# Mixing layers of a hybrid stack: four split weight pieces begun a layer ahead instead of two, and two high parts kept in the tiles of the attention's turned weights

## The chip, the cores and the metric

One core of a Trainium2 chip runs one program. The metric is the time of the device in microseconds (us); of several executions the median is given. PE is TensorE, DVE VectorE, ACT ScalarE, POOL GpSimd, SP SyncE.

## The reference, cut to what matters

The reference is a stack of four token mixers (attention, mLSTM, HGRN2, attention) on 272 tokens, and then two blocks on 256 tokens, each of which mixes tokens and then applies a feed-forward part. The change lies at the entry of the two mixing parts:

```python
for l in range(DEPTH_2):                     # 2
    h = rmsnorm_2(x, g_pre_mix[l])
    z = jnp.einsum('bsd,de->bse', h, w_in[l])
    ...                                      # z is split; MoBA, FoX, MLA and dilated attention
    y = jnp.einsum('bse,ed->bsd', mix, w_out[l])
    x = x + rmsnorm_2(y, g_post_mix[l])
    h = rmsnorm_2(x, g_pre_ffn[l])
    f = jax.nn.silu(h @ w_gate[l]) * (h @ w_up[l])
    x = x + rmsnorm_2(f @ w_down[l], g_post_ffn[l])
```

All is float32. `D_MODEL` is 1024.

## The kernel before, in words

**Layers.** The program runs the layers a0, b, c, a3 and then M0, F0, M1, F1: a mixing layer M and a feed-forward layer F for each of the two blocks (`layer_mix` builds M). Activations lie with features on partitions: `HT` holds the residual stream as eight tiles of 128 features by tokens, k = 0 to 7.

**Precision.** Each float32 operand is split into a high part, rounded to float32r, and a low part, the rest. A product takes three matmuls: high weights by high activations (L402), high by low (L403), low by high (L404). The activations' parts are `XH` (an ACT instruction, L545) and `XL` (DVE, L533), one pair for each k.

**The stream of weights.** All weights are one stream of chunks, cut into pieces of 128 x 1024 (512 KB), numbered p; p0 below is the first piece of a mixing layer. A piece is split in one of two ways.

- From a raw copy: SP loads it to `wraw` (L258, 3 buffers), ACT casts it to the high part `whi` (L389), DVE subtracts to get the low part `wlo` (L395).
- "Parted": `begin_part` has POOL load the float32r copy `whi` (L329); `finish_part` has ACT write its negative to `wlo` (L336) and POOL add the piece from memory to it in the transfer (L337).

There are 7 buffers of `whi` (`WH`) and 5 of `wlo` (`WB`). The function `ahead` decides, at each piece, which parted pieces are begun and finished: `far, few, fewer = FAR` lets pieces up to 9 ahead be begun while at most 2 are begun or made, and one be finished early.

**A mixing layer.** Its first chunks, p0 and p1, and p2 and p3, go the way from a raw copy; chunk 3 does as well, but into tiles called `MH` and `ML`; from p6 on the pieces are parted. The generator `together` runs the first four products as one: for each k, the high parts of p0 to p3 by XH (4 matmuls), by XL (4), then the low parts by XH (4); 96 matmuls in all (L1576). All pieces of chunks 1 and 2 are in use until its last k. After it come the products of chunk 3 (`MH`, `ML`), then those of p6, p7 and so on.

**The norm at the entry.** M0 follows the last attention layer, whose last out-projection tiles are added to `HT` (DVE, L966). M1 follows F0: DVE computes the reciprocal root `RP`, PE spreads it, DVE scales `Y` (L1526), the sum goes into `HT` (L1527, k = 0 on DVE, the others on POOL), ACT makes XH, DVE makes XL. In both, ACT squares `HT` to `nsq` (L480), POOL adds these up (M0: L491 into `nsa`; M1: L485), and a few matmuls sum over features (M0: L495 and L496; M1: L456). In M0 their result scales the products; the products do not wait for it.

**Order.** The order on an engine is that in which the program issues the instructions, by a list of due times; each waits by semaphores for its operands and buffers. POOL issues its transfers in the same order as its additions.

**The attention's turned weights.** Later in a mixing layer `attend` keeps the transposed attention weights in two tiles, `pT0` and `pT1`, of 3 KB a partition together, two buffers each.

Of the kernel before, what the change touches and what calls it, by code (L numbers as in the profile page):

```python
# [9 lines left out]
F32 = mybir.dt.float32  # L10
F32R = mybir.dt.float32r
# [7 lines left out]
P = 128  # L19
# [40 lines left out]
WR, WH = 3, 7  # L60
HI_AHEAD, LO_AHEAD, FAR = 5, 3, (9, 2, 1)
PB = {"mm": 3, "s": 2, "t": 1, "g": 1, "a": 1}
# [161 lines left out]
def kernel(ctx: ExitStack, tc: tile.TileContext, xt: bass.AP, pos: bass.AP, small: bass.AP,  # L224
# [86 lines left out]

    parted, n_, off_, p_ = [], 0, 0, 0
    for i_, (t_, kt_, nt_) in enumerate(seq):
        first_ = i_ == 0 or t_ in ("bg", "c", "a3", "i0", "f0", "i1", "f1") and t_ != seq[i_ - 1][0] and seq[i_ - 1][0][:2] != "up"
        n_ = 1 if first_ else n_ + 1
        w_ = _cols(kt_, nt_)
        for x_, c0_ in enumerate(range(0, w_, SUB * P)):
            if POOL(t_, n_, x_) and not (n_ in MORE and t_[0] in MT):
                parted.append((p_, off_, w_, c0_, min(w_, c0_ + SUB * P)))
            p_ += 1  # L320
        off_ += P * w_
# [18 lines left out]
    def ahead(p, hold):  # L340


        far, few, fewer = FAR
        while parted and parted[0][0] <= p:
            begin_part()
        while begun and (begun[0][0] <= (p if hold else p + LO_AHEAD) or begun[0][0] <= p + far and not hold and len(made_lo) < fewer):
            finish_part()
        while parted and not hold and (parted[0][0] <= p + HI_AHEAD or parted[0][0] <= p + far and len(begun) + len(made_lo) < few):
            begin_part()
# [12 lines left out]
    def chunk(tag, into=None, more_due=False):  # L362
# [6 lines left out]
        for c0 in range(0, n, SUB * P):  # L369
# [11 lines left out]
            elif more:  # L381
                hi, lo = (t[:, c0:c0 + SUB * P] for t in acc["more"])
            else:
                hi = wp.tile([P, SUB * P], F32R, name="whi", bufs=WH)
                lo = wp.tile([P, SUB * P], F32R, name="wlo", bufs=WB)
# [1145 lines left out]
    def layer_mix(l, upd):  # L1531
# [3 lines left out]
        with tc.tile_pool(name=f"M{l}", bufs=2, reuse_waits="tile") as wk:  # L1535
            acc["more"] = [t.rearrange("p a b -> p (a b)") for t in mview(wk, 8, S)]
            Rf, _ = norm_in(wk, "gpm", 8 * l, NM, upd, CUT_S if upd else None)
            R = Rf[:, NM:]
# [160 lines left out]
            def attend(kind, mt, p, qf, vt):  # L1699
                pts = [wk.tile([P, 2, S], F32, name="pT0"), wk.tile([P, 2, P], F32, name="pT1")]  # L1700

# [436 lines left out]
```

## Time and profile before

| | |
|---|---|
| Median of 3 runs | 1419.31 us (1416.23 to 1421.89) |
| The profiled execution | 1422.77 us |
| Its span, first to last instruction | 1421.0 us |
| Mean granted TensorE clock | 0.993 |
| Busy: PE, DVE, ACT, POOL | 95%, 70%, 57%, 31% |

Times in the rows below are counted from the start of the span of that one execution. The time outside the span is 1.8 us. M0's `together` runs from 752.96 to 766.73, M1's from 1086.74 to 1098.67.

### The profile page before, as it was taken

To read this page: it belongs to the slowest core of one execution; us is meant where nothing else is said; L and a number is where in the kernel's file an instruction comes from. 1 tells how busy PE (TensorE), PEld (TensorE's weight loads), DVE (VectorE), ACT (ScalarE), POOL (GpSimd) and SP (SyncE) were. 2 spreads that over 40 slices of the span, in tenths; PEclk is the share of its full clock that TensorE was granted. 3 is DMA by queue.
4 is the path that set the end of the run, shared out by engine and by line. 5 is a ranking of instruction groups with operands and counts; after the bars stand their busy time and mean duration, and the time that the engine had idled before them with its cause. 6 is when DMAs were issued, how large, how long until landed. Compare 5 with 4: busy or idle time off the path is not lost.

```text
span 1421.0 us, 27398 instructions
## 1 busy us (share of the span) xinstructions
PE 1356.4 (95%) x10347; PEld 1261.1 (89%) x10347; DVE 992.2 (70%) x2424; ACT 804.6 (57%) x1700; POOL 446.6 (31%) x611
## 2 busy tenths in 40 slices
PE   6999999999899999998999999999999899999997
PEld 5878989999899888898778888999999789899986
DVE  5865569999776767687656676787645576687744
ACT  6875655556644454448675586454444667455532
POOL 3322468778703434123224511300014340400000
PEclk9999999999999999999999999999999999999999
DMA  9989999999568988559889973456564994466662
GB/s 275 283 186 209 230 242 247 231 238 242 135 185 234 253 180 196 134 179 247 191 171 237 259 193 104 144 189 195 180 198 151 265 239 125 119 193 194 186 184 89
DMA packets 79349, 281.88 MB, mean 198 GB/s; under 512 B 9024, under 2 KB 10184, under 8 KB 79216
## 3 DMA queue, kind: packets, MB, share of 16 engines
q0 software_dynamic: 44512, 160.74, 49.0%
q1 hardware_dynamic: 34272, 118.60, 26.0%
q8 instruction: 81, 1.33, 0.4%
q10 hardware_dynamic: 432, 0.79, 0.1%
q14 instruction: 52, 0.43, 0.1%
HBM read 279.01 MB, written 1.07 MB: 197 GB/s over the span
## 4 chain that ended last, share of the span: by engine, by line
PE 72%; DVE 10%; DMA 6%; ACT 5%; issue 4%; POOL 2%; SPq 0%; DVEq 0%; POOLq 0%; ACTq 0%
PE pmm L402 14%; PE pmm L403 14%; PE pmm L404 14%; DMA wraw<-in_wts_dram 2%; PE ps L404 2%; PE ps L403 2%; PE ps L402 2%; DVE wlo L395 2%; DMA wlo<-in_wts_dram 2%; PE ps L838 1%; DMA whi<-in_wts_dram 1%; PE pa L878 1%; PE ps L1270 1%; PE pt L863 1%; PE pmm L1893 1%
## 5 line engine op out<-in xcount | busy, mean ns | idle before, releaser
L402 PE MATMUL pmm<-XH,whi 128*128 128x272 f32 (+1 forms) x1544 | 458.1, 298 | 17.5 <-ACT whi L389 10.8
L404 PE MATMUL pmm<-XH,wlo 128*128 128x272 f32 (+1 forms) x1544 | 444.8, 289 | 8.5 <-DMA wlo<-in_wts_dram 7.9
L403 PE MATMUL pmm<-XL,whi 128*128 128x272 f32 (+1 forms) x1544 | 445.4, 289 | 2.6 <-DVE XL L533 2.6
L389 ACT CAST whi<-wraw 128x1024 fp32r<-128x1024 f32 (+1 forms) x211 | 217.8, 1033 | 242.5 <-DMA wraw<-in_wts_dram 180.4
L395 DVE TENSOR_TENSOR wlo<-wraw,whi 128x1024 fp32r<-128x1024 f32 (+1 forms) x211 | 256.5, 1217 | 96.5 <-PE pmm L404 43.3
L402 PEld LDWEIGHTS pmm<-XH,whi 128*128 128x128 f32 x1544 | 294.4, 191 | 31.7 <-ACT whi L389 10.8
L404 PEld LDWEIGHTS pmm<-XH,wlo 128*128 128x128 f32 x1544 | 294.9, 191 | 10.0 <-DMA wlo<-in_wts_dram 8.5
L403 PEld LDWEIGHTS pmm<-XL,whi 128*128 128x128 f32 x1544 | 295.0, 191 | 4.4 <-DVE XL L533 3.7
L336 ACT ACTIVATE wlo<-whi 128x1024 fp32r<-128x1024 f32 (+1 forms) x150 | 157.9, 1054 | 86.4 <-PE pmm L404 39.8
L337 POOL DMA_DIRECT2D wlo<-in_wts_dram x150 | 130.5, 873 | 212.3 <-ACT wlo L336 101.1
L402 PE MATMUL pmm<-MH,whi 128*128 128x256 f32 (+1 forms) x624 | 182.3, 292 | 0.6 <-DVE HT L966 0.6
L329 POOL DMA_DIRECT2D whi<-in_wts_dram x150 | 89.5, 598 | 296.7 <-PE pmm L404 235.9
L403 PE MATMUL pmm<-ML,whi 128*128 128x256 f32 (+1 forms) x624 | 177.9, 285 | 1.5 <-DVE ML L586 0.8
L404 PE MATMUL pmm<-MH,wlo 128*128 128x256 f32 (+1 forms) x624 | 177.3, 284 | 0.0
L402 PEld LDWEIGHTS pmm<-MH,whi 128*128 128x128 f32 x624 | 117.7, 189 | 7.8 <-issue 6.2
L403 PEld LDWEIGHTS pmm<-ML,whi 128*128 128x128 f32 x624 | 117.9, 189 | 2.2 <-DVE ML L586 1.1
L404 PEld LDWEIGHTS pmm<-MH,wlo 128*128 128x128 f32 x624 | 118.1, 189 | 0.0
L404 PE MATMUL ps<-XH,wlo 128*128 128x256 f32 (+1 forms) x256 | 72.5, 284 | 1.4 <-DVE wlo L395 1.4
L403 PE MATMUL ps<-XL,whi 128*128 128x256 f32 (+1 forms) x256 | 72.9, 285 | 0.0
L402 PE MATMUL ps<-XH,whi 128*128 128x256 f32 (+1 forms) x256 | 72.0, 283 | 0.0
L404 PEld LDWEIGHTS ps<-XH,wlo 128*128 128x128 f32 x256 | 48.7, 190 | 1.6 <-DVE wlo L395 1.6
L403 PEld LDWEIGHTS ps<-XL,whi 128*128 128x128 f32 x256 | 48.4, 189 | 0.0
(933 smaller groups left out, 2870.2 us busy)
## 6 DMA issues: line engine op xcount, KB each, us to landing
wraw<-in_wts_dram SPq DMA_DIRECT2D x209, 512.0 KB, 4.4
whi<-in_wts_dram POOLq DMA_DIRECT2D x148, 512.0 KB, 6.4
wlo<-in_wts_dram POOLq DMA_DIRECT2D x148, 512.0 KB, 7.8
wraw<-in_wts_dram SPq DMA_DIRECT2D x16, 384.0 KB, 3.5
nb<-drb POOLq DMA_DIRECT2D x8, 272.0 KB, 6.4
HT<-in_xt_dram SPq DMA_DIRECT2D x4, 272.0 KB, 9.7
nb<-drf POOLq DMA_DIRECT2D x8, 128.0 KB, 4.9
whi<-in_wts_dram POOLq DMA_DIRECT2D x2, 384.0 KB, 6.9
```

Of the source, the lines that this page charges most:

```text
L329: nc.gpsimd.dma_start(hi[:, :c1 - c0], src)
L336: act(lo[:, :w], hi[:, :w].bitcast(F32), AF.Copy, scale=-1.0)
L337: nc.gpsimd.dma_start(lo[:, :w], src, accum_op=ALU.add)
L389: nc.scalar.copy(hi[:, :c1 - c0], raw[:, :c1 - c0])
L395: V.tensor_tensor(lo[:, :c1 - c0], raw[:, :c1 - c0], hi[:, :c1 - c0].bitcast(F32), op=ALU.subtract)
L402: PE.matmul(ps, c.hi(b), xh, start=first, stop=False)
L403: PE.matmul(ps, c.hi(b), xl, start=False, stop=False)
L404: PE.matmul(ps, c.lo(b), xh, start=False, stop=last)
L838: PE.matmul(sv, qp[:, n, qs], kp[:, :, k0:k1], start=True, stop=False)
L863: PE.transpose(pt[:c1 - c0, (2 * y + x) * P:(2 * y + x + 1) * P], p_[:, x, c0:c1], K["ident"])
L878: PE.matmul(po[64 * x:64 * x + 64, :], vt[:kk, bq - 1 + y, 64 * x:64 * x + 64], pT[:kk, y, x].rearrange("p n t -> p (n t)"), start=y == 0, ...
L1270: PE.matmul(sl[:, 0:P], s["kw"], halves_of(kq, CB_[0], T + CA[0], b), start=True, stop=True)
```

## The change

The rule `FAR` becomes a pair: where the next piece to be begun belongs to a mixing layer (its tags begin with "i" or "u"), four pieces instead of two may be begun or made. Those begun take `whi` buffers while the layer ahead still runs. The high parts of chunk 2 (p2 and p3) no longer take `whi` buffers: they go into two tiles of the mixing layer's own pool, named `pT`, 4 KB a partition each. `attend` takes its two tiles of turned weights as views of one such tile.

```diff
--- before.py
+++ after.py
@@ -58,7 +58,7 @@
 WB = 5
 DV, UPP = (), True
 WR, WH = 3, 7
-HI_AHEAD, LO_AHEAD, FAR = 5, 3, (9, 2, 1)
+HI_AHEAD, LO_AHEAD, FAR = 5, 3, {False: (9, 2, 1), True: (9, 4, 1)}
 PB = {"mm": 3, "s": 2, "t": 1, "g": 1, "a": 1}
 BLOCKS = ((0, 16), (16, 144), (144, 272))
 CMASK = 7 * P + 64
@@ -309,7 +309,7 @@
                 tag[:2] == "up" and UPP or tag == "b" and (n, x) in B_PL or tag == "c" and n >= 3 and n % C_PN in C_PM or tag[0] == "f" and (n, x) in PF)
 
 
-    parted, n_, off_, p_ = [], 0, 0, 0
+    parted, mixing, n_, off_, p_ = [], set(), 0, 0, 0
     for i_, (t_, kt_, nt_) in enumerate(seq):
         first_ = i_ == 0 or t_ in ("bg", "c", "a3", "i0", "f0", "i1", "f1") and t_ != seq[i_ - 1][0] and seq[i_ - 1][0][:2] != "up"
         n_ = 1 if first_ else n_ + 1
@@ -317,6 +317,8 @@
         for x_, c0_ in enumerate(range(0, w_, SUB * P)):
             if POOL(t_, n_, x_) and not (n_ in MORE and t_[0] in MT):
                 parted.append((p_, off_, w_, c0_, min(w_, c0_ + SUB * P)))
+                if t_[0] in "iu":
+                    mixing.add(p_)
             p_ += 1
         off_ += P * w_
     begun, made_lo = [], {}
@@ -340,9 +342,9 @@
     def ahead(p, hold):
 
 
-        far, few, fewer = FAR
         while parted and parted[0][0] <= p:
             begin_part()
+        far, few, fewer = FAR[bool(parted) and parted[0][0] in mixing]
         while begun and (begun[0][0] <= (p if hold else p + LO_AHEAD) or begun[0][0] <= p + far and not hold and len(made_lo) < fewer):
             finish_part()
         while parted and not hold and (parted[0][0] <= p + HI_AHEAD or parted[0][0] <= p + far and len(begun) + len(made_lo) < few):
@@ -381,7 +383,10 @@
             elif more:
                 hi, lo = (t[:, c0:c0 + SUB * P] for t in acc["more"])
             else:
-                hi = wp.tile([P, SUB * P], F32R, name="whi", bufs=WH)
+                if tag[0] == "i" and state["n"] == 2:
+                    hi = acc["big"]()
+                else:
+                    hi = wp.tile([P, SUB * P], F32R, name="whi", bufs=WH)
                 lo = wp.tile([P, SUB * P], F32R, name="wlo", bufs=WB)
             with ExitStack() as es:
                 if (tag, state["n"], c0 // (SUB * P)) in HELD and "last" in acc:
@@ -1534,6 +1539,8 @@
         X = (XH, XL)
         with tc.tile_pool(name=f"M{l}", bufs=2, reuse_waits="tile") as wk:
             acc["more"] = [t.rearrange("p a b -> p (a b)") for t in mview(wk, 8, S)]
+
+            acc["big"] = lambda: wk.tile([P, SUB * P], F32R, name="pT", bufs=2)
             Rf, _ = norm_in(wk, "gpm", 8 * l, NM, upd, CUT_S if upd else None)
             R = Rf[:, NM:]
             mixed = []
@@ -1697,7 +1704,9 @@
                 fl.later(D_VT, turn)
 
             def attend(kind, mt, p, qf, vt):
-                pts = [wk.tile([P, 2, S], F32, name="pT0"), wk.tile([P, 2, P], F32, name="pT1")]
+                big = acc["big"]().bitcast(F32)
+                pts = [big[:, :2 * S].rearrange("p (x t) -> p x t", x=2),
+                       big[:, 2 * S:2 * S + 2 * P].rearrange("p (x t) -> p x t", x=2)]
 
                 def scores(b):
                     nk = P * (b + 1)
```

The count of instructions is the same on every engine. What moves lies at the entries of M0 and M1. The L-numbers of the changed kernel are higher by two to seven there (L331 is L329, L339 is L337, L338 is L336, L394 is L389, L400 is L395, L550 is L545, L538 is L533, L1583 is L1576, L1531 and L1532 are L1526 and L1527).

**First place: the entry of M0.** POOL there, before: two high parts begun in the layer a3, a third and fourth only when two are used, the low part of p6 after two additions, then four high parts ahead of the low parts of p7 and of those behind it.

```order
L329 DMA whi<-in_wts_dram 128x1024
L337 DMA wlo<-in_wts_dram 128x1024 x2
L329 DMA whi<-in_wts_dram 128x1024 x2
L491 TENSOR_TENSOR nsa<-nsq 128x256
L491 TENSOR_TENSOR nsa<-nsq,nsa 128x256
L337 DMA wlo<-in_wts_dram 128x1024
L491 TENSOR_TENSOR nsa<-nsq,nsa 128x256 x4
L329 DMA whi<-in_wts_dram 128x1024 x4
L337 DMA wlo<-in_wts_dram 128x1024 x4
L329 DMA whi<-in_wts_dram 128x1024
```

And in the changed kernel:

```order
L331 DMA whi<-in_wts_dram 128x1024
L339 DMA wlo<-in_wts_dram 128x1024
L331 DMA whi<-in_wts_dram 128x1024 x3
L496 TENSOR_TENSOR nsa<-nsq 128x256
L496 TENSOR_TENSOR nsa<-nsq,nsa 128x256 x3
L339 DMA wlo<-in_wts_dram 128x1024
L496 TENSOR_TENSOR nsa<-nsq,nsa 128x256 x2
L331 DMA whi<-in_wts_dram 128x1024 x2
L339 DMA wlo<-in_wts_dram 128x1024 x4
L331 DMA whi<-in_wts_dram 128x1024
```

Two of the high parts moved from behind the additions to ahead of them; two, not four, now stand ahead of the low part of p7. The low part of p6 moved behind two more additions.

ACT at the same place, before: the casts of p1, p2, p3 stand among the XH of the entry, the three squares behind them.

```order
L389 CAST whi<-wraw 128x1024
L545 ACTIVATE XH<-HT,sm 128x256 x2
L389 CAST whi<-wraw 128x1024
L545 ACTIVATE XH<-HT,sm 128x256 x3
L480 ACTIVATE nsq<-HT 128x256 x3
L545 ACTIVATE XH<-HT,sm 128x256
L336 ACTIVATE wlo<-whi 128x1024
L389 CAST MH<-wraw 128x1024 x2
L545 ACTIVATE XH<-HT,sm 128x256
L480 ACTIVATE nsq<-HT 128x256 x5
```

And in the changed kernel:

```order
L394 CAST whi<-wraw 128x1024
L550 ACTIVATE XH<-HT,sm 128x256
L394 CAST whi<-wraw 128x1024
L550 ACTIVATE XH<-HT,sm 128x256 x5
L485 ACTIVATE nsq<-HT 128x256 x3
L394 CAST pT<-wraw 128x1024 x2
L394 CAST MH<-wraw 128x1024
L550 ACTIVATE XH<-HT,sm 128x256
L485 ACTIVATE nsq<-HT 128x256 x3
L338 ACTIVATE wlo<-whi 128x1024
L485 ACTIVATE nsq<-HT 128x256
L394 CAST MH<-wraw 128x1024
```

The casts of p2 and p3, now into `pT`, moved behind the three squares, the second cast into `MH` behind the low part of p6 and a square.

**Second place: the entry of M1.** DVE there, before: nothing but the norm, since the low parts of p2 and p3 are made ahead of it.

```order
L449 SCALAR_TENSOR_TENSOR RP<-RP 128x2
L1526 SCALAR_TENSOR_TENSOR Y<-Y,sm,pg 128x256
L1527 TENSOR_TENSOR HT<-HT,Y 128x256
L1526 SCALAR_TENSOR_TENSOR Y<-Y,sm,pg 128x256 x2
L533 SCALAR_TENSOR_TENSOR XL<-HT,sm,XH 128x256
L1526 SCALAR_TENSOR_TENSOR Y<-Y,sm,pg 128x256
```

And in the changed kernel:

```order
L454 SCALAR_TENSOR_TENSOR RP<-RP 128x2
L1531 SCALAR_TENSOR_TENSOR Y<-Y,sm,pg 128x256
L400 TENSOR_TENSOR wlo<-wraw,pT 128x1024
L1532 TENSOR_TENSOR HT<-HT,Y 128x256
L1531 SCALAR_TENSOR_TENSOR Y<-Y,sm,pg 128x256 x2
L400 TENSOR_TENSOR wlo<-wraw,pT 128x1024
L538 SCALAR_TENSOR_TENSOR XL<-HT,sm,XH 128x256
L1531 SCALAR_TENSOR_TENSOR Y<-Y,sm,pg 128x256
```

The two subtractions moved into the chain from Y to HT and to XL.

PE towards the end of `together` in M1, before: the matmuls that sum the squares (L456) stand behind the first product with `MH`.

```order
L1576 MATMUL pmm<-XL,whi 128x256 x3
L1576 MATMUL ps<-XL,whi 128x256
L1576 MATMUL pmm<-XH,wlo 128x256 x3
L1576 MATMUL ps<-XH,wlo 128x256
L402 MATMUL ps<-XH,MH 128x256
L403 MATMUL ps<-XL,MH 128x256
L404 MATMUL ps<-XH,ML 128x256
L456 MATMUL pa<-ones,nsq 128x1 x4
L402 MATMUL ps<-XH,MH 128x256
L403 MATMUL ps<-XL,MH 128x256
```

And in the changed kernel, where L461 is L456 and L1583 is L1576:

```order
L1583 MATMUL ps<-XH,wlo 128x256
L1583 MATMUL pmm<-XH,whi 128x256 x2
L1583 MATMUL pmm<-XH,pT 128x256
L461 MATMUL pa<-ones,nsq 128x1 x4
L1583 MATMUL ps<-XH,pT 128x256
L1583 MATMUL pmm<-XL,whi 128x256 x2
L1583 MATMUL pmm<-XL,pT 128x256
L1583 MATMUL ps<-XL,pT 128x256
L1583 MATMUL pmm<-XH,wlo 128x256 x3
L1583 MATMUL ps<-XH,wlo 128x256
L1583 MATMUL pmm<-XH,whi 128x256 x2
L1583 MATMUL pmm<-XH,pT 128x256
```

The sums moved from behind `together` into it, behind 75 of its 96 matmuls. In M0 they moved ahead by 22: behind 68 of the 96 instead of 90.

## Rows read from the trace of the kernel before

**Rows 1.** The page, part 1: busy us (share of the span) and instructions of each engine.
```profile
PE 1356.4 (95%) x10347; PEld 1261.1 (89%) x10347; DVE 992.2 (70%) x2424; ACT 804.6 (57%) x1700; POOL 446.6 (31%) x611
```

**Rows 2.** Waits of PE, whole run: us in total, times, longest.
```profile
PE pmm L404 <- DMA wlo<-in_wts_dram: 7.9, 3, 5.2
```

**Rows 3.** Timeline of PE around 778 and 1114: start, duration, [idle before <-releaser].
```profile
778.00 0.38 PE L404 MATMUL pmm<-XH,wlo 128*128 128x256 f32 x1 [2.32 <-DMA wlo<-in_wts_dram]
...
1114.31 0.58 PE L404 MATMUL pmm<-XH,wlo 128*128 128x256 f32 x1 [5.19 <-DMA wlo<-in_wts_dram]
```

**Rows 4.** Windows: busy us (instructions) of each engine, granted clock, DMA share, GB/s.
```profile
710.00:715.00 5.00, 3.13 (x21) 2.26 (x20) 3.31 (x15) 3.87 (x14) 1.41 (x2) 1.00 0.80 183
770.00:775.00 5.00, 5.00 (x44) 5.00 (x44) 4.16 (x12) 3.25 (x8) 1.72 (x2) 1.00 1.08 280
775.00:780.00 5.00, 2.68 (x21) 2.48 (x20) 3.12 (x8) 4.35 (x8) 1.41 (x2) 0.95 1.06 211
780.00:785.00 5.00, 5.00 (x33) 5.00 (x33) 3.27 (x8) 3.81 (x8) 1.41 (x2) 0.71 1.07 247
1110.00:1115.00 5.00, 0.69 (x3) 0.69 (x4) 3.50 (x10) 4.82 (x11) 1.91 (x3) 0.90 1.08 220
1115.00:1120.00 5.00, 5.00 (x35) 5.00 (x35) 1.83 (x6) 2.93 (x5) 0.61 (x2) 0.76 1.06 231
```

**Rows 5.** Timeline of POOL at the end of together, M0 and M1.
```profile
765.50 2.20 POOL L329 DMA_DIRECT2D whi<-in_wts_dram  x4 [1.94 <-PE pmm L1576]
...
1095.06 3.38 POOL L485 TENSOR_TENSOR nsq<-nsq 128x256 f32<-128x256 f32 x3
1098.38 2.16 POOL L329 DMA_DIRECT2D whi<-in_wts_dram  x4
```

**Rows 6.** Source view of L337: issues at 767.9, at 1100.5, and all 150.
```profile
DMA to landing us min/median/max: 10.0/10.0/10.0
...
DMA to landing us min/median/max: 13.8/13.8/13.8
...
DMA to landing us min/median/max: 5.3/7.8/15.7
```

**Rows 7.** Source view of L329: the four issues from 765.5, the four from 1098.4.
```profile
DMA to landing us min/median/max: 3.7/6.7/8.4
...
DMA to landing us min/median/max: 7.3/10.2/11.8
```

**Rows 8.** Timeline of ACT, then PE, at the entry of M0.
```profile
749.62 1.05 ACT L389 CAST whi<-wraw 128x1024 fp32r<-128x1024 f32 x1 [2.52 <-DMA wraw<-in_wts_dram]
753.04 1.03 ACT L480 ACTIVATE nsq<-HT 128x256 f32<-128x256 f32 x3 [0.57 <-PE pmm L403]
...
754.24 0.78 PE L1576 MATMUL pmm<-XH,whi 128*128 128x256 f32 x2 [0.99 <-DVE HT L966]
755.80 0.28 PE L1576 MATMUL ps<-XH,wlo 128*128 128x256 f32 x1
```

**Rows 9.** Timeline of DVE, then PE, at the entry of M1.
```profile
1081.67 1.23 DVE L395 TENSOR_TENSOR wlo<-wraw,whi 128x1024 fp32r<-128x1024 f32 x1 [0.93 <-PE pmm L404]
1085.20 0.48 DVE L1526 SCALAR_TENSOR_TENSOR Y<-Y,sm,pg 128x256 f32<-128x256 f32 x1 [0.81 <-PE pg L463]
1086.84 0.78 DVE L533 SCALAR_TENSOR_TENSOR XL<-HT,sm,XH 128x256 fp32r<-128x256 f32 x1
...
1082.11 0.71 PE L520 MATMUL pa<-ones,nsl 128*128 128x128 f32 x4 [0.53 <-ACT nsl L507]
1086.74 0.62 PE L1576 MATMUL pmm<-XH,whi 128*128 128x256 f32 x3 [1.57 <-ACT XH L545]
1087.68 0.50 PE L1576 MATMUL pmm<-XL,whi 128*128 128x256 f32 x2 [0.21 <-DVE XL L533]
```

**Rows 10.** Source view of L258 on SP: the raw loads of 740:762, of 1080:1090.
```profile
DMA to landing us min/median/max: 4.4/5.4/8.4
...
DMA to landing us min/median/max: 4.2/5.3/6.3
```

## The prediction

> **What bounds the kernel.** I read the page's busy times first: PE is busy 95% of the span [rows 1], so a change that adds no work can win only where PE stands idle or runs slowly. Next the waits of PE: those on a low part that came by transfer are 7.9 us in three, the longest 5.2 [rows 2]. The timeline of PE finds the two that lie in mixing layers: 2.32 us up to 778.00 in M0 and 5.19 us up to 1114.31 in M1 [rows 3]. Both are the first matmul with the low part of p7, the second parted piece. The windows show what follows each: at the full clock 5 us hold 44 matmuls, but 780 to 785 holds 33 at a granted clock of 0.71, and 1115 to 1120 holds 35 at 0.76 [rows 4]. A share between 0.5 and 1 means that a part of the window ran at 1.2 instead of 2.4 GHz.
>
> **Why p7 is late.** The four low buffers of chunks 1 and 2 stay taken until `together` ends, and p6 has the fifth. So ACT can write p7's negative only after the end of `together`, and POOL issues its low transfer behind four high ones of 512 KB, issued in M0 from 765.50 and in M1 from 1098.38 [rows 5]. The low transfer then took 10.0 us and 13.8 us, where the median of 150 is 7.8 and the shortest 5.3 [rows 6]. The four high ones land one after another. The first took 3.7 us and the last, issued 1.65 us later (three of the four 0.55 us issues in the row of 2.20), 8.4; so (8.4 + 1.65 - 3.7) / 3 = 2.1 us lie between two landings, and in M1 likewise (11.8 + 1.62 - 7.3) / 3 = 2.0 [rows 5, 7].
>
> **The most there is to win.** The waits are 2.3 + 5.2. The slow clock: in M0 the windows lack 11 matmuls from 780 and some 2.6 before it (2.68 us of busy time would hold 23.6, not 21), at 5.00 / 44 = 0.114 us each 1.5 us; in M1 9 and some 3.1 (0.69 us would hold 6.1), 1.4 us [rows 4]. In all 10.4 us. Each following term is a loss or gain on PE's own path, as PE goes from `together` through the products without other long waits in these stretches.
>
> **Part 1: two fewer transfers ahead of p7's low part.** It should land after its issue sooner by 2 x 2.1 = 4.2: 5.8 us in M0, 9.6 in M1. From the other side it lands no sooner than the shortest, 5.3, and, if the number ahead doesn't matter, as before (10.0 and 13.8). I take 6.8 in M0, between 5.8 and the median 7.8, and 9.6 in M1, where even the first high part took 7.3. Issue and use both shift with the end of `together`, so only the landing time counts: M0's wait of 2.3 shrinks by 3.2, to nothing; M1's 5.2 shrinks by 4.2, to 1.0. **Gain: 2.3 and 4.2.** With waits of that size I expect no slow clock behind them: the stretch 710 to 715, with PE busy 3.13 of 5 us, kept 1.00 [rows 4]. **Gain: 1.5 and 1.4.** The two high parts that moved forward are transfers of a stretch in which POOL issues little; in M0 they lie ahead of the layer's additions beside low parts of a3, for which PE shows no wait now. I count nothing, and up to 2.1 us each if one of those has less slack than one landing.
>
> **Part 2: p2 and p3 in `pT`, entry of M0.** The memory of `pT` is free only with the layer ahead, so the two casts now stand behind the three squares, which wait for PE's last out-projection and run from 753.04 for 1.03 us. A cast takes 1.05 us, so they end at 755.1 and 756.2 [rows 8]. DVE's two subtractions (1.23 us each [rows 9]) end at 756.4 and 757.6. The fourth low matmul of k = 0, at 755.80 before [rows 8], waits until 757.6: **loss 1.8 us**, of which the high matmuls' waits are a part. It would be nothing only if the squares ran earlier, which PE's order forbids. The raw loads take 4.4 to 8.4 us here [rows 10], and those for p3 and `MH` start later, when three raw tiles go round; p3's is hidden unless it takes the longest, since the squares hold its cast anyway.
>
> **Part 3: entry of M1.** Here the norm's chain DVE, PE, DVE, ACT, PE is what PE waits for (1.57 us to 1086.74, then XL to 1087.68). Before, the last subtraction (1081.67 to 1082.90) was done ahead of it [rows 9]. Now one stands between Y of k = 0 (from 1085.20, 0.48 us) and HT, and one ahead of XL. The chain's first step waits for sums that PE makes from 1082.11 for 0.71 us [rows 9], so without the subtraction ahead of it it starts 0 to 0.7 earlier; I take 0.2, since it began at the end of both. XH then comes 1.2 - 0.2 = 1.0 later and XL 2 x 1.2 - 0.2 = 2.2 later. PE needs XL at its fifth matmul, so it loses what XL loses, less a little that neighbouring instructions overlap: **loss 2.0 us** (1.0 if only XH's delay counted, which PE's order rules out; 2.4 at the most).
>
> **Part 4: the sums inside `together`.** PE reaches them after 68 (M0) or 75 (M1) matmuls and waits for the last square or its addition. In M1 POOL's additions ended at 1095.06 + 3.38 = 1098.4 [rows 5]. They follow Y and shift by some 1.0, to about 1099.4; PE is there at 1087.7 + 2.0 + 71 x 0.114 = 1097.8. That is 1.6; **loss 1.2**, since POOL now puts an addition into a stretch in which it waits for Y (bounds 0 and 2.2). In M0 the last square stands behind the second cast into `MH`, whose raw load starts when p2's subtraction frees a tile, about 756.4; it lands 4.4 to 8.4 later [rows 10], and with a cast of 1.05 and a square of 0.4 behind it the square ends at 762.3 to 766.3. PE is there at 757.6 + 60 x 0.114 = 764.4. **Loss 0 to 1.9; I take 0.7**: the median landing (5.4) gives none, but this load meets POOL's transfer of p6's low part.
>
> **Sum.** M0: -2.3 - 1.5 + 1.8 + 0.7 = -1.3. M1: -4.2 - 1.4 + 2.0 + 1.2 = -2.4. Together -3.7 us, on the profiled execution 1422.8 to 1419.1. That execution lies 3.5 us above the median of the runs; on the median 1419.3 becomes **1415.6 us**, a change of -0.26%. About 0.5% (7.1 us) is what a measurement of this kernel can tell from no change.
>
> **Rival A, the full gain.** The entry costs hide (chunk 3's pieces or the later products take up what the entry loses, or the casts come sooner than I place them), and waits and slow clock go: up to -10.4 and with half the entry cost -7.5, so 1409 to 1412. For it: PE has slack in ACT and DVE over most of the layer. Against it: the entry waits stand ahead of everything PE does in the layer.
>
> **Rival B, the slow clock moves to the entries.** Each entry now has two bursts of idle time within some 4 us, each burst over 1 us. Then 1.5 + 1.4 come back: 1415.6 + 2.9 = 1418.5, no change. Against it is the window 710 to 715 at 1.00 with 1.9 us idle; for it, that behind the 2.32 us of M0 the clock did fall [rows 3, 4]. The Trainium skill (TensorE: Matmul & The Clock Gate, "What's actually happening") says that the gate sets the rate by how busy PE has been recently. The fall after both p7 waits agrees with it; by that rule the scattered idle time of an entry counts as one long wait does, which is this rival.
>
> **Rival C, slower.** The landing of p7's low part hangs on what all queues ask of the DMA engines, not on how many pieces stand ahead. The DMA share is 1.06 to 1.09 in these stretches [rows 4]: the engines are full whoever asks. Then it lands 10.0 and 13.8 us after an issue that is later, the waits and the slow clock stay, and the entry costs remain: +1.8 + 0.7 + 2.0 + 1.2 = +5.7, 1425.0 us. It turns slower than before where the landings gain less than some 1.5 us each. The Trainium skill (DMA: Bandwidth & Descriptors, "Issuing engines are not separate DMA queues") has a rule that speaks for it: transfers of all issuing engines run on the same 16 engines and interleave. By it raw loads of SP, which now come later, share with p7. Against it the spacing of 2.1 us between POOL's landings shows that its own pieces go one by one, so two fewer must count for something.
>
> **Chances.** My forecast with 1412.5 to 1418 has 0.50, A 0.22, B 0.14, C 0.14. The range 1409.5 to 1424 takes in most of A, B and the part of C in which the landings gain a little; the forecast's own range is 1412.5 to 1418. Faster by over 0.5% (below 1412.2) comes from A and a little of the forecast, 0.26; slower by over 0.5% (above 1426.4) needs C with the upper bounds of part 4, 0.07; the rest, 0.67, lies within.
>
> **What would show it.** In the changed profile: two issues of L331, not four, before the first L339 at the end of `together`; the wait of L409 on a low part near 0 in M0 and 1 in M1; the windows behind them at a clock of 1.00. At the entries, the first low matmuls of `together` 1.8 and 2.0 us later against the last matmul of the layer ahead; L400 on `pT` between L1531 and L1532. A wait of PE at L461 of about 1 in M1. I am wrong if p7's low transfer still takes over 9 and 12 us, if the clock falls at an entry, or if a3's low parts make PE wait around 745.

## The result, and the profile after

The changed kernel takes 1427.85 us (median of 5 runs, 1426.26 to 1430.51), the kernel before 1419.31. The ratio on record, of all the runs and not of the two medians, is 1.0053, 95% interval 1.0029 to 1.0076: it is slower by 0.5%. The forecast was 1415.6 us, with a range from 1409.5 to 1424. The profiled execution took 1428.57 us (span 1426.8, mean granted clock 0.988), 5.8 us more than that of before. The medians differ by 8.5 us; the trace of before lies 3.5 us above its median and that of the changed kernel 0.7 above its own, so the traces hold 5.8 of the 8.5 us.

PE's busy time grew by 4.9 us for the same 10347 matmuls [rows 1]: part of the loss is matmuls at the slow clock. The page, part 1:

```profile
PE 1361.3 (95%) x10347; PEld 1264.5 (89%) x10347; DVE 994.2 (70%) x2424; ACT 803.5 (56%) x1700; POOL 445.4 (31%) x611
```

Waits of PE over the whole run (us in total, times, longest). L409 answers to L404 of [rows 2]:

```profile
PE pt L1753 <- ACT pT L1756: 5.9, 2, 3.9
...
PE pmm L1583 <- ACT XH L550: 2.6, 1, 2.6
PE pmm L409 <- DMA wlo<-in_wts_dram: 2.2, 3, 1.3
...
PE pmm L1583 <- DVE XL L538: 1.9, 1, 1.9
...
PE pmm L1583 <- ACT pT L394: 1.7, 1, 1.7
```

The wait on low parts fell from 7.9 to 2.2, as forecast (1.3 of the 2.2 is at another place than p7). The first line is new: PE's transposes of attention weights (L1753) wait for ACT's copies of the turned weights (L1756). The timeline of PE shows where each wait stands:

```profile
755.13 0.38 PE L1583 MATMUL pmm<-XH,pT 128*128 128x256 f32 x1 [1.70 <-ACT pT L394]
756.08 0.39 PE L1583 MATMUL ps<-XH,pT 128*128 128x256 f32 x1 [0.57 <-ACT pT L394]
...
779.21 0.39 PE L409 MATMUL pmm<-XH,wlo 128*128 128x256 f32 x1 [0.39 <-DMA wlo<-in_wts_dram]
...
800.07 0.66 PE L1753 MATMUL pt<-ce,p__10306 128*128 128x128 f32 x4 [1.99 <-ACT pT L1756]
...
1088.80 0.50 PE L1583 MATMUL pmm<-XH,whi 128*128 128x256 f32 x2 [2.58 <-ACT XH L550]
1091.41 0.80 PE L1583 MATMUL pmm<-XL,whi 128*128 128x256 f32 x2 [1.88 <-DVE XL L538]
...
1114.56 0.38 PE L409 MATMUL pmm<-XH,wlo 128*128 128x256 f32 x1 [0.49 <-DMA wlo<-in_wts_dram]
...
1137.27 1.11 PE L1753 MATMUL pt<-ce,p__14453 128*128 128x128 f32 x4 [3.88 <-ACT pT L1756]
```

And the windows (columns as in [rows 4]):

```profile
755.00:760.00 5.00, 4.20 (x19) 3.71 (x20) 4.71 (x4) 4.55 (x9) 2.60 (x3) 0.67 0.71 225
775.00:780.00 5.00, 4.61 (x39) 4.41 (x38) 3.61 (x10) 4.85 (x11) 0.55 (x1) 1.00 1.08 220
780.00:785.00 5.00, 5.00 (x45) 5.00 (x44) 3.92 (x10) 3.74 (x7) 2.85 (x4) 1.00 1.06 211
...
800.00:805.00 5.00, 4.93 (x22) 3.73 (x22) 3.16 (x17) 2.69 (x8) 2.24 (x3) 0.66 1.08 285
...
1090.00:1095.00 5.00, 3.59 (x18) 3.59 (x19) 4.37 (x9) 3.21 (x7) 5.00 (x6) 0.66 0.48 156
...
1115.00:1120.00 5.00, 5.00 (x45) 5.00 (x44) 4.02 (x11) 4.71 (x9) 2.87 (x4) 1.00 1.06 210
...
1140.00:1145.00 5.00, 5.00 (x34) 4.62 (x34) 2.98 (x12) 3.14 (x8) 1.82 (x4) 0.76 1.08 278
```

Behind p7 the clock is now 1.00 (0.71 and 0.76 before). It falls instead at both entries and behind both new waits.

**Where the time went.** For a place in PE's program I subtract the start of a matmul in the trace of before from that of the same matmul here, and take differences between places. The places, by their start before: 752.7, 766.5, 783.4, 809.0, 1072.1, 1100.5, 1120.7, 1148.7, and the end. In us, + is lost, one profiled execution each; the e-numbers are the experiments below.

| kernel | M0 entry | M0 p7 | M0 behind p7 | to F0's end | M1 entry | M1 p7 | M1 behind p7 | F1 |
|---|---|---|---|---|---|---|---|---|
| changed | +3.1 | -3.4 | +3.6 | -1.9 | +3.7 | -6.2 | +7.0 | 0.0 |
| e1 | +2.7 | -3.4 | +1.9 | -1.6 | +4.1 | -6.2 | +4.9 | +1.7 |
| e2 | +2.8 | -3.3 | +4.1 | +0.3 | +5.9 | -6.0 | +4.6 | 0.0 |
| e3 | -0.5 | +1.9 | +0.2 | -0.1 | +3.2 | -3.7 | +0.9 | 0.0 |
| e4 (control) | -0.9 | -0.1 | -0.9 | -0.3 | +0.6 | +1.2 | 0.0 | -0.1 |
| e5 | +3.1 | -3.3 | +1.1 | +0.6 | +3.7 | -5.8 | +2.0 | +0.1 |
| e6 | -0.7 | -4.1 | +5.4 | +0.8 | +2.1 | -6.8 | +9.2 | 0.0 |
| e7 | +3.2 | -3.4 | +2.3 | -0.3 | +5.0 | -5.3 | +2.2 | +1.5 |
| e8 (control) | -0.9 | -1.8 | -0.1 | -1.7 | +1.6 | -1.2 | 0.0 | +1.6 |
| e9 | -0.3 | -4.1 | +4.7 | -1.7 | 0.0 | -6.8 | +10.3 | +0.9 |
| e10 | +4.9 | -4.1 | +5.4 | +0.6 | +9.1 | -7.0 | +3.8 | 0.0 |
| e11 | +2.7 | -3.4 | +0.6 | +0.3 | +4.0 | -6.1 | +0.8 | 0.0 |
| e12 | +2.0 | -3.4 | -0.2 | -1.9 | +6.5 | -5.5 | +4.6 | +1.5 |

In the changed kernel the entries and p7 together give -0.3 in M0 and -2.5 in M1. What is new is the loss behind p7, 3.6 + 7.0. The -1.9 comes mostly from the entry of F0, where the clock was slow in the execution of before only. The columns add up to +5.9; the two executions differ by 5.8. The two controls (the kernel before with the edit of e1 or of e5), whose times do not differ from before, show how far one execution scatters: up to 1.8 us in a column. The 3.6 alone would not stand far above that; the 7.0 does, and the waits of 2.0 and 3.9 us are in neither before nor the controls.

**The new wait.** The gates of a mixing layer pass through memory: POOL writes `drf`, and when that has landed it loads it back four times as `nb`. POOL's timeline in M0, after:

```profile
782.06 0.56 POOL L1669 DMA_DIRECT2D drf<-fg  x1
782.61 0.57 POOL L331 DMA_DIRECT2D whi<-in_wts_dram  x1
783.49 0.89 POOL L339 DMA_DIRECT2D wlo<-in_wts_dram  x1 [0.32 <-ACT vt L1701]
790.80 2.18 POOL L1671 DMA_DIRECT2D nb<-drf  x4 [6.43 <-DMA drf<-fg]
792.93 0.59 POOL L331 DMA_DIRECT2D whi<-in_wts_dram  x1
...
1127.34 2.19 POOL L1671 DMA_DIRECT2D nb<-drf  x4 [7.37 <-DMA drf<-fg]
```

And before:

```profile
785.29 0.56 POOL L1662 DMA_DIRECT2D drf<-fg  x1 [1.18 <-DVE fg L1660]
785.84 0.58 POOL L329 DMA_DIRECT2D whi<-in_wts_dram  x1
789.27 0.88 POOL L337 DMA_DIRECT2D wlo<-in_wts_dram  x1 [2.85 <-ACT wlo L336]
789.82 0.88 POOL L329 DMA_DIRECT2D whi<-in_wts_dram  x1
...
794.44 2.22 POOL L1664 DMA_DIRECT2D nb<-drf  x4 [3.03 <-DMA drf<-fg]
```

Before, two high parts (785.84 and 789.82) went out while `drf` was on its way. Now only an earlier piece does, and the piece that was issued at 785.84 stands behind `nb`: POOL idles 6.43 us (7.37 in M1) and issues it at 792.93, 7.1 us later (7.7 in M1). It lands at 798.60 instead of 795.29, in M1 at 1135.79 instead of 1130.48. ACT's timeline shows who needs it:

```profile
798.70 1.06 ACT L338 ACTIVATE wlo<-whi 128x1024 fp32r<-128x1024 f32 x1 [3.86 <-DMA whi<-in_wts_dram]
799.66 0.35 ACT L1756 COPY pT<-pt 128x256 f32<-128x256 f32 x1
...
1135.90 1.06 ACT L338 ACTIVATE wlo<-whi 128x1024 fp32r<-128x1024 f32 x1 [5.76 <-DMA whi<-in_wts_dram]
```

ACT stands at the negative of a piece that PE first uses at 817.56, some 19 us later; the copy of the turned weights, which PE waits for at 800.07 and 1137.27, is the next instruction in ACT's order. Two engines that work in order each stand at an operand that arrives late, and work that is due now is queued behind. Before, ACT came to the same negative at 795.36 after 0.62 us:

```profile
795.36 1.06 ACT L336 ACTIVATE wlo<-whi 128x1024 fp32r<-128x1024 f32 x1 [0.62 <-PE pt L1744]
```

Behind POOL's stop in M1 the DMA engines had less to do: their share was 0.90 from 1125 to 1130 and 0.86 from 1130 to 1135, where before had 1.09 and 1.05. The late landing there does not come from full engines. The second of these windows, the changed kernel first:

```profile
1130.00:1135.00 5.00, 3.20 (x25) 2.97 (x25) 2.57 (x10) 0.14 (x2) 4.70 (x9) 1.00 0.86 197
```

```profile
1130.00:1135.00 5.00, 5.00 (x40) 4.48 (x39) 4.29 (x20) 2.59 (x5) 3.12 (x6) 1.00 1.05 270
```

### The profile page after: what moved, and what is told of

It is laid out like the page before. It is cut to its first block, busy times and chain, and to the rows that moved or that the text cites. A ratio compares the mean times of both kernels' runs of the same rounds, so it can differ in the third digit from the quotient of the medians.

```text
span 1426.8 us, 27397 instructions
## 1 busy us (share of the span) xinstructions
PE 1361.3 (95%) x10347; PEld 1264.5 (89%) x10347; DVE 994.2 (70%) x2424; ACT 803.5 (56%) x1700; POOL 445.4 (31%) x611
## 4 chain that ended last, share of the span: by engine, by line
PE 73%; DVE 11%; issue 5%; ACT 5%; DMA 4%; POOL 3%; SPq 0%; DVEq 0%; POOLq 0%; ACTq 0%
PE pmm L407 14%; PE pmm L408 14%; PE pmm L409 14%; PE ps L409 2%; PE ps L408 2%; PE ps L407 2%; DVE wlo L400 2%; PE ps L843 1%; DMA whi<-in_wts_dram 1%; DMA drf<-fg 1%; PE pmm L1583 1%; PE pa L883 1%; POOL wlo L339 1%; PE ps L1275 1%; PE pt L868 1%
## 5 line engine op out<-in xcount | busy, mean ns | idle before, releaser
L409 PE MATMUL pmm<-XH,wlo 128*128 128x272 f32 (+1 forms) x1544 | 444.3, 288 | 2.6 <-DMA wlo<-in_wts_dram 2.2
L394 ACT CAST whi<-wraw 128x1024 fp32r<-128x1024 f32 (+1 forms) x207 | 213.6, 1032 | 232.6 <-DMA wraw<-in_wts_dram 164.9
L400 DVE TENSOR_TENSOR wlo<-wraw,whi 128x1024 fp32r<-128x1024 f32 (+1 forms) x207 | 251.4, 1215 | 92.1 <-ACT whi L394 38.2
L409 PEld LDWEIGHTS pmm<-XH,wlo 128*128 128x128 f32 x1544 | 294.7, 191 | 3.9 <-DMA wlo<-in_wts_dram 2.8
L338 ACT ACTIVATE wlo<-whi 128x1024 fp32r<-128x1024 f32 (+1 forms) x150 | 157.5, 1054 | 90.3 <-PE pmm L409 45.2
L339 POOL DMA_DIRECT2D wlo<-in_wts_dram x150 | 130.3, 869 | 196.8 <-ACT wlo L338 87.2
L331 POOL DMA_DIRECT2D whi<-in_wts_dram x150 | 89.9, 600 | 316.6 <-PE pmm L409 236.0
L409 PE MATMUL pmm<-MH,wlo 128*128 128x256 f32 (+1 forms) x624 | 177.8, 285 | 0.0
L409 PEld LDWEIGHTS pmm<-MH,wlo 128*128 128x128 f32 x624 | 118.5, 190 | 0.0
L409 PE MATMUL ps<-XH,wlo 128*128 128x256 f32 (+1 forms) x256 | 72.2, 283 | 1.4 <-DVE wlo L400 1.4
L409 PEld LDWEIGHTS ps<-XH,wlo 128*128 128x128 f32 x256 | 48.3, 189 | 1.6 <-DVE wlo L400 1.6
L550 ACT ACTIVATE XH<-HT,sm 128x272 fp32r<-128x272 f32 (+1 forms) x64 | 31.6, 512 | 30.3 <-DVE HT L971 13.5
```

The lines of the kernel that those rows point to most:

```text
L331: nc.gpsimd.dma_start(hi[:, :c1 - c0], src)
L338: act(lo[:, :w], hi[:, :w].bitcast(F32), AF.Copy, scale=-1.0)
L339: nc.gpsimd.dma_start(lo[:, :w], src, accum_op=ALU.add)
L394: nc.scalar.copy(hi[:, :c1 - c0], raw[:, :c1 - c0])
L400: V.tensor_tensor(lo[:, :c1 - c0], raw[:, :c1 - c0], hi[:, :c1 - c0].bitcast(F32), op=ALU.subtract)
L409: PE.matmul(ps, c.lo(b), xh, start=False, stop=last)
```

## The experiments

My theory: the loss is these two stops, POOL at `nb` and ACT at a far piece's negative. The rivals: the entries with their slow clock cost what was lost; the free `whi` buffers or the number in `FAR` make the stream worse by themselves. Ratios are against the kernel before, run beside each.

**e1: the four loads of `nb` on SP**, in the changed kernel; **e4: the same in the kernel before**, as a control.

```diff
-                    nc.gpsimd.dma_start(nb[:, h], dr[h:h + 1].to_broadcast([P, S]))
+                    nc.sync.dma_start(nb[:, h], dr[h:h + 1].to_broadcast([P, S]))
```

> The changed kernel with the four small loads of the gates' rows (nb from drf) issued by SP instead of POOL; nothing else differs. Theory 1: the two new waits of PE on the turned weights' copies (2.0 us in M0, 3.9 us in M1) come from POOL, which stands at these four loads until drf has landed (6.4 and 7.4 us) with high parts of weights queued behind. Then both waits and the slow clock behind them go: 1417 to 1421 us, 6 to 10 us under the changed kernel's 1427.9. Theory 2: the copies on ACT are late because the DMA engines are full and the high parts land late whoever issues them: 1426 to 1429 us, the waits stay at 1.5 to 4 us. Either way the entries keep their cost: L1583 waits for XH 2.6 and XL 1.9 in M1, for pT 2.3 in M0.

> Before with the four small loads of the gates' rows issued by SP instead of POOL: the control for the first kernel. Theory 1: in before these loads stand behind more high parts and cost PE nothing, so the time is before's within 2 us, 1417 to 1421 us. Theory 2: POOL's standing at them costs something in before too: 3 us or more faster.

e1: 1425.42 us, ratio 1.0033 (1.001 to 1.0056), between the ranges of the two theories. e4: 1420.63, 1.0006 (0.9991 to 1.0022), as theory 1 has it. The loss behind p7 fell from 3.6 to 1.9 and from 7.0 to 4.9, and the wait of L1753 on the copies went down to below 0.5. But another took its place; the timelines of PE and of ACT in e1:

```profile
804.49 0.44 PE L1700 MATMUL pt<-ce,vr 128*128 128x128 f32 x2 [1.15 <-ACT pT L1758]
...
1139.55 0.48 PE L1700 MATMUL pt<-ce,vr 128*128 128x128 f32 x2 [2.00 <-ACT pT L1758]
```

```profile
1137.60 1.06 ACT L338 ACTIVATE wlo<-whi 128x1024 fp32r<-128x1024 f32 x1 [2.73 <-issue]
...
1139.12 0.37 ACT L1758 COPY pT<-pt 128x256 f32<-128x256 f32 x1
```

ACT stands at the negative of the next far piece, whose high part landed at 1137.53, and a later copy is behind it. By these rows POOL's stop is a part of the cause, not the whole.

**e2: only the tiles.** The changed kernel with two begun pieces also for mixing layers. **e3: only the number**, (9, 3, 1) for mixing layers, with p2 and p3 in `whi` as before. The edit of e2:

```diff
-HI_AHEAD, LO_AHEAD, FAR = 5, 3, {False: (9, 2, 1), True: (9, 4, 1)}
+HI_AHEAD, LO_AHEAD, FAR = 5, 3, {False: (9, 2, 1), True: (9, 2, 1)}
```

> The changed kernel with FAR at (9, 2, 1) for all pieces: only the place of the two high parts in pT is left. Theory 1: what lets high parts be begun early is the two buffers that chunk 2 leaves free, not the number in FAR; four high parts are then issued ahead of the entry of M0 all the same, two remain ahead of p7's low part, and the time is that of the changed kernel, 1425 to 1430 us. Theory 2: the number in FAR does it; then p7's waits return (2.3 and 5.2 us) on top of the entries' cost, 1433 to 1437 us.

> Before with FAR at (9, 3, 1) for mixing layers and no pT: three high parts may be begun ahead, as many as the seven buffers hold beside the four of chunks 1 and 2. Theory 1 (buffers decide): the order is before's but for a swap, and so is the time, 1417 to 1422 us, p7's waits near 2.3 and 5.2. Theory 2 (the number decides): one high part fewer ahead of p7's low part, its waits shorter by up to 2.1 each with no cost at the entries, 1413 to 1416 us.

e2: 1432.07 us, 1.009 (1.0058 to 1.0121), 2 us above the range of theory 1. e3: 1424.87, 1.004 (1.0024 to 1.0056), above both ranges. In e2 POOL still loads four high parts ahead of M0's entry and two ahead of p7's low part, and both new waits are there (2.0 and 2.3 us). So the two `whi` buffers that the tiles set free do the moving; the four in `FAR` is not needed for the loss. That the number costs nothing by itself is not shown: three in e3 cost 0.4% without the tiles. There the waits at p7 stay (3.1 and 3.0), and in M1 PE waits 1.0 us more for POOL's sums; why it loses as much as 0.4% is not settled by that.

**e5: ACT's stop taken away.** The negatives of the 10th and 11th parted piece of a mixing layer are issued behind the copies of the turned weights (`late` numbers the parted pieces of a layer). **e8: the same in the kernel before.** **e11: e5 and e1 together.**

```diff
+            if late.get(p, 0) in (10, 11) and "ptc" in acc:
+                es.enter_context(tc.issue_after(acc["ptc"]))
             act(lo[:, :w], hi[:, :w].bitcast(F32), AF.Copy, scale=-1.0)
...
-                    nc.scalar.copy(pts[0][:, :, b * P:(b + 1) * P], ptv[:, 0])
+                    acc["ptc"] = nc.scalar.copy(pts[0][:, :, b * P:(b + 1) * P], ptv[:, 0]).ins
                     if b == 1:
-                        nc.scalar.copy(pts[1], ptv[:, 1])
+                        acc["ptc"] = nc.scalar.copy(pts[1], ptv[:, 1]).ins
```

> The changed kernel with two negations in each mixing layer (of the tenth and eleventh parted piece, which PE needs 15 us later or more) put behind the first three copies of turned weights on ACT. Theory 3: ACT takes its instructions in order and stands at such a negation until the piece's high part has landed, and the copies that PE waits for stand behind it; POOL's stop at the gates' loads only made that landing later. Then PE's waits on these copies (in the changed kernel 2.0 and 3.9 us, with a slow clock behind them, 3.6 and 6.4 us in all) go to under 0.5, and the time is 1418 to 1422 us. Theory 2: the transfers as a whole are behind, and PE then waits for low parts of weights instead, 1.5 us or more in each layer: 1424 to 1428 us.

> Before with the same two negations in each mixing layer put behind the copies: the control. In before their high parts land before ACT comes to them or within 0.7 us, so theory 3 expects no change, 1417 to 1422 us; a gain of 3 us or more would say that the order helps by itself.

> The changed kernel with both edits of before: the two far negations behind the copies on ACT, and the gates' loads on SP. Theory 3 (ACT's stop is the cause, POOL's only what brought it about): little more than the hold alone, 1422 to 1426 us, PE without waits over 1 us on copies of turned weights. If the two stops add up: 1418 to 1421 us.

e5: 1425.34 us, 1.0032 (1.0017 to 1.0048). e8: 1420.22, 0.9991 (0.9972 to 1.001), as expected. e11: 1421.93, 1.0011 (0.9995 to 1.0027), between its two ranges. By its time e5 lies where theory 2 had put it, but the sign of theory 2 is not there: PE waits for low parts 0.5 us in M0 and 1.0 in M1, and for the copies less than 0.3, as theory 3 had it. Of the changed kernel's 0.53%, the hold takes back 0.21, the move to SP 0.20, both 0.42. The intervals of such differences are some 0.3 to either side, so only the 0.42 is clear of noise, and the split between the two is not. In the kernel before neither makes a difference that can be measured. In e11 the loss behind p7 is 0.6 and 0.8 us. This settles the cause: the two stops are most of the slowdown, by the best estimate four fifths, with the interval from a quarter to all of it. With them gone the change is worth nothing that the measurement can tell; that its entries and p7 still give -0.7 and -2.1 in the trace is hardly more than the scatter of the controls.

**e6: p7's low part first, with no new buffers.** In the kernel before, the 4th to 7th high part of a mixing layer go behind the newest low part on POOL. **e9: that with the hold of e5.**

```diff
+            if 4 <= late.get(p, 0) <= 7 and "plo" in acc:
+                es.enter_context(tc.issue_after(acc["plo"]))
+            nc.gpsimd.dma_start(hi[:, :c1 - c0], src)
...
-        nc.gpsimd.dma_start(lo[:, :w], src, accum_op=ALU.add)
+        acc["plo"] = nc.gpsimd.dma_start(lo[:, :w], src, accum_op=ALU.add).ins
```

> Before, no pT and FAR as it was; only the transfers of the fourth to seventh high part of a mixing layer are put behind the latest low part on POOL, so that at most one of the four stands ahead of p7's low part. If the number of pieces ahead in POOL's queue sets p7's landing, p7's waits fall from 2.3 and 5.2 to under 1 without any cost at the entries. By theory 3 PE then reaches the attention 4 to 6 us sooner against the transfers, and waits 1 to 3 us for the copies of turned weights behind a far negation: 1415 to 1420 us. If theory 3 is wrong, nothing takes the place of the waits: 1410 to 1414 us.

> Both edits on before: low part first, and the two far negations behind the copies. Theory 3: p7's waits and the copies' waits both go, 1410 to 1415 us. Theory 2 (transfers as a whole behind): PE waits for low parts of p9 to p12 instead, 1416 to 1421 us.

e6: 1427.46 us, 1.0055 (1.0035 to 1.0076). e9: 1425.88, 1.0037 (1.002 to 1.0053). Both are misses, above every range that was expected. Here p7's waits go without any cost at M0's entry, and the columns for p7 show the whole prize, 4.1 and 6.8. Then 5.4 and 9.2 are lost. The timelines of ACT, DVE and PE in M0 of e6:

```profile
773.14 1.06 ACT L342 ACTIVATE wlo<-whi 128x1024 fp32r<-128x1024 f32 x1 [4.82 <-PE pt L1699]
```

```profile
776.40 0.42 DVE L1663 SCALAR_TENSOR_TENSOR fg<-fg,fe 32x256 f32<-32x256 f32 x1 [4.67 <-ACT fe L1662]
```

```profile
781.89 0.49 PE L1699 MATMUL pt<-ce,vr 128*128 128x128 f32 x2 [2.75 <-DVE vr L1691]
```

The high part that now comes later landed at 773.06, 9.0 us after its issue. ACT stands at its negative until 773.14 (the releaser that the row names had long been done), the gates' exponentials are behind it, DVE stands 4.67 us at `fg`, `vr` is behind that, and PE waits for `vr`; then the clock is 0.71. This is the same form in a third place. The hold of e5 doesn't reach these pieces, so e9 loses likewise.

**e10: p2's and p3's low parts, not the high ones, in `pT`**, and `FAR` at (9, 3, 3) for mixing layers. Then p7's negative need not wait for the end of `together` at all.

```diff
-HI_AHEAD, LO_AHEAD, FAR = 5, 3, {False: (9, 2, 1), True: (9, 4, 1)}
+HI_AHEAD, LO_AHEAD, FAR = 5, 3, {False: (9, 2, 1), True: (9, 3, 3)}
...
-                    hi = acc["big"]()
+                    lo = acc["big"]()
```

> The changed kernel with the low parts of chunk 2, not the high ones, in the two pT tiles, and FAR at (9, 3, 3) for mixing layers. Two low buffers come free, so the low parts of p7 and p8 are asked for before together ends; the high parts of p2 and p3 keep their early casts. If p7's wait comes from the low buffers that together holds, p7's waits go altogether, and each entry loses only what two late subtractions cost (0 to 1.5 us in M0, 2 to 4 in M1). By theory 3 a far negation on ACT may still stop PE later, 1 to 5 us in all: 1414 to 1421 us. If the transfers as a whole are behind (theory 2), PE waits for the low parts of p9 to p12 instead, 1.5 us or more in each layer: 1419 to 1425 us.

1435.61 us, 1.0103 (1.0076 to 1.013), the slowest and above both ranges. PE no longer waits at p7, and waits longer at the entries and behind p7. Two things differ from the changed kernel here, so this run does not tell which of them costs. Waits of PE in e10:

```profile
PE pt L1753 <- ACT pT L1756: 3.6, 1, 3.6
...
PE pa L525 <- ACT nsl L512: 2.5, 1, 2.5
PE pmm L1583 <- DVE HT L971: 2.5, 1, 2.5
```

**e7: M1's two subtractions behind XL of k = 0**, with the hold of e5.

```diff
+                elif tag[0] == "i" and state["n"] == 2 and "lo0" in acc:
+                    es.enter_context(tc.issue_after(acc["lo0"]))
```

> The changed kernel with the far negations held, and at the entry of M1 the two subtractions from pT put behind XL of k = 0 on DVE. If their place in the chain is what the entry of M1 costs, XH comes about 1.2 us and XL about 2.4 us sooner, the low parts of k = 0 at the same time as in the changed kernel; the idle time is in fewer pieces, PE loses 0.5 to 1.5 us less than the changed kernel between the last matmul of F0 and the end of together (3.9 to 4.4 us there), and M0's entry stays as it is: 1421 to 1425 us.

1426.72 us, 1.0057 (1.0036 to 1.0078): a miss, since 1421 to 1425 was expected. XH comes after 1.57 us of waiting, as before, but then PE waits 0.71 and 1.28 us for the low parts themselves and the entry costs 5.0 instead of 3.7. The two subtractions cost their place in DVE's order at both places that were tried.

**e12: e11 with matmuls that nobody reads in the entries' gaps**, to see what the slow clock there costs. The table's keys are the block, k, the row of products and the product that they stand ahead of.

```diff
+WARM_AT = {(0, 0, 0, 2): 11, (0, 0, 0, 3): 3, (1, 0, 0, 0): 17, (1, 0, 1, 0): 9}
...
+                                for _ in range(warm):
+                                    PE.matmul(pw[:, :P], ones, ones, start=True, stop=True)
```

> The changed kernel with both stops taken away (negatives of far pieces held behind the copies of the turned weights, the loads of nb on SP), and with matmuls of the ones that nobody reads put into the entry gaps: 11 and 3 ahead of the third and fourth matmul of M0's together, 17 ahead of its first and 9 ahead of its fifth in M1. They fill gaps in which PE waits anyway. Theory (the slow clock behind the entries is the price of the scattered idle time): the stretches behind the entries, which granted 0.66 and 0.67, show 1.00 or nearly; the two entries lose some 1.2 and 1.5 us less, since about 10 and 15 matmuls stood 0.21 us apart and not 0.118; the kernel comes out near 1419. Rival (the clock falls there for another reason, or the added matmuls delay what they stand ahead of): the stretches stay below 0.8, the entries cost the same 2.7 and 4.3 us or more, and the time is that of the kernel without them, 1421 to 1423.

1426.1 us, 1.0042 (1.0024 to 1.006). The windows of e12 (the first holds 43 matmuls, not 19, the filler among them):

```profile
755.00:760.00 5.00, 5.00 (x43) 4.68 (x42) 3.97 (x4) 5.00 (x9) 2.53 (x4) 1.00 0.72 206
...
1090.00:1095.00 5.00, 5.00 (x42) 5.00 (x41) 3.82 (x9) 3.14 (x9) 4.83 (x6) 0.92 0.01 3
```

The clock part held in M0: 1.00 where it was 0.67. In M1 it is 0.92 where it was 0.66, but 0.74 in the window ahead, 1085 to 1090, where the changed kernel had 1.00: the slow stretch only moved forward. From XL on M1's `together` loses next to nothing (e11 loses 1.7 there). The time did not follow. Each f32 filler is two matmul records, so there was twice what I meant, and in M1 the 17 stood ahead of matmuls of the norm itself: the entry cost 6.5 instead of 4.0. Behind p7 of M1, 4.6 were lost; the timelines of POOL, ACT and PE:

```profile
1136.98 0.84 POOL L1741 TENSOR_SCALAR tb<-nb,cumT 128x128 f32<-128x128 f32 x1 [7.82 <-ACT p__14622 L1748]
...
1138.83 1.14 POOL L334 DMA_DIRECT2D whi<-in_wts_dram  x2
```

```profile
1142.28 0.84 ACT L344 ACTIVATE wlo<-whi 128x768 fp32r<-128x768 f32 x1 [5.13 <-PE pmm L415]
```

```profile
1144.76 0.58 PE L1640 MATMUL pg<-ones,sq 128*128 128x1 f32 x4 [2.00 <-DVE lu L1652]
```

The high part of ACT's piece was issued only at 1138.83 and landed at 1142.17. POOL had stood 7.82 us at the first addition that reads `nb`, whose first row, loaded by SP, landed at 1136.79; the exponentials that the row names ended at 1136.89. So POOL's stop can come back when only the loads are moved to SP: what reads them is still in its order. By e11 less e12 in M0 (2.7 - 2.0), and by the 1.7 in M1, a smaller filler in the right place may be worth 0.7 to 1.7 us an entry. That is an estimate, no larger than the scatter of the controls, and it was not tried.

## Why the prediction was wrong

**What bounds the kernel, and p7: right.** e6 shows that the prize at p7 is 4.1 and 6.8 us; I had 3.8 (2.3 + 1.5) and 6.6 (5.2 + 1.4).

**Part 1 (two fewer transfers ahead): right, sizes a little off.** The source view of L339 for p7's issue in M0, and for it and the next in M1 (the shorter is p7's):

```profile
DMA to landing us min/median/max: 8.1/8.1/8.1
...
DMA to landing us min/median/max: 8.6/9.4/10.1
```

Against 10.0 and 13.8 [rows 6] the landing gained 1.9 and 5.2; I had 3.2 and 4.2. The waits are 0.39 and 0.49 (forecast 0 and 1.0), and the clock behind them is 1.00.

**Parts 2 and 3 (the entries' waits): right in kind, part 3 too small; part 4 (the sums): wrong.** The waits for the casts are 1.70 + 0.57, and at M0's fourth low matmul PE is 1.9 us late (forecast 1.8). At the first XL of M1 it is 2.7 late (forecast 2.0, at most 2.4). At the sums inside `together` PE waits under 0.1 in either layer, not 0.7 and 1.2. (In M0 the forecast counted 60 matmuls up to them; behind the twelfth of 68 there are 56, which moves only a bound, by 0.5.) What stands in their place is rival B's mechanism: the clock is 0.67 and 0.66 behind the entries, where 5 us hold 19 and 18 matmuls. That the clock falls at an entry was one of the forecast's own signs of being wrong. The totals, 3.1 lost in M0 (forecast 1.8 + 0.7) and 3.7 in M1 (2.0 + 1.2), came near by luck: one term stood in for another. The Trainium skill (TensorE: Matmul & The Clock Gate, "What's actually happening") has the rate follow how busy PE has been recently; the fall at the entries of this trace and the 1.00 of e12's M0 agree, though like waits did not always end alike (see the last section).

**The sum for what I priced: -3.7, measured -0.3 - 2.5 = -2.8.** That is not where the forecast failed.

**The step that failed** is the sentence behind the most there is to win: "PE goes from `together` through the products without other long waits in these stretches", with the words on the change, "what moves lies at the entries of M0 and M1". The second was not so: with two buffers free and other numbers begun, POOL's order also moved behind p7, where the gates' `nb` went ahead of a high part. The forecast priced POOL's order up to p7's low part and nothing behind it. The first was true of the trace of before only. It left 3.6 + 7.0 us out, the largest loss in either layer.

**Rival C** ended on the right side for the wrong reason: its landings did shorten. No rival named a stop behind p7. (The DMA shares in [rows 4] are 1.06 to 1.08; the 1.09 of the forecast stands in windows behind them.) What speaks for its premise: the three low parts that follow p7 in M1 landed within 0.3 us of before (1116.96 against 1116.73 for the first), though PE was 5 us late before them and 1 us early behind. But POOL began its transfers there 5.9 us later (1104.32 against 1098.38) with two pieces fewer ahead (4.0 us by the spacing of 2.0), and its first piece took 5.5 us instead of 7.3: that by itself comes to about the same. In e6 and e9 time won ahead was lost at the next piece that had not landed, which their edit had also made later. That the stream of pieces sets the pace of this stretch fits these runs; it was not tested by itself (a kernel with fewer bytes there would). It does not explain the loss in the changed kernel's M1, where the DMA share fell to 0.86 behind POOL's stop.

**Open:** e3's loss; how the loss divides between the two stops; and what a place as in the last paragraph would give with fewer bytes.

## What to carry to other kernels

When a change frees buffers or lets transfers start earlier, compare the whole order of each queue to the end of the layer, not the place that was meant: one issue that slips behind a waiting instruction on an in-order engine is late by that whole wait. A far-ahead preparation on a shared engine (here a negation of a piece due 19 us later) must not stand ahead of work that is due now; where its operand is a transfer, ask when it lands. Time won ahead of a transfer may be only lent, as e6 and e9 suggest: look for the next piece that has not landed.

## What was not expected of the hardware

The same wait does not always slow the clock. PE's wait of 1.87 us at one place of a3, with the same instructions, stands in all fourteen traces. The clock stayed at 1.00 behind it in seven of them (before [rows 4], e1, e2, e6, e8, e11 and e12) and fell in seven (the changed kernel, e3, e4, e5, e7, e9 and e10). Windows of two that fell, the changed kernel and e5:

```profile
710.00:715.00 5.00, 3.75 (x15) 3.09 (x16) 2.92 (x16) 2.85 (x14) 0.85 (x1) 0.73 0.79 168
```

```profile
715.00:720.00 5.00, 5.00 (x23) 4.02 (x22) 2.38 (x13) 1.75 (x8) 0.01 (x1) 0.66 0.71 126
```

It cost some 1.7 us each time. At F1's entry the same wait of 1.65 us left the clock at 1.00 in eleven traces and was followed by a fall in e1, e7 and e12 (0.73 in the window of e12). So a row at 1.00, as the one on which my part 1 rested, does not show that a wait of this size is free.

A few KB through memory took as long as a large piece here: `drf`, issued at 782.06 and 1117.96, let `nb` go at 790.80 and 1127.34, 8.7 and 9.4 us later, where 512 KB pieces took 5.3 to 15.7 [rows 6]. The queue took the time, not the size: in all fourteen traces the transfers that POOL issued in M0 and in M1 landed in the order of their issue, and `drf` landed 0.15 to 0.21 us behind the piece issued just ahead of it, each of the 28 times (in the changed kernel at 790.52 behind 790.35, and at 1127.06 behind 1126.89). Moving the loads of `nb` to SP left this wait as it was, since the write stayed in POOL's queue; a run with the write elsewhere was not made.
